# Two 8x8 triangular inverses at once, and the block below them by two products, in place of one 16-step substitution

## The chip, the cores and the metric

The kernel runs on one core of one Trainium2 chip. The time is device time in microseconds (us) from one launch, and the median of the runs is compared. Below, TensorE is PE, VectorE is DVE, ScalarE is ACT, GpSimd is POOL and SyncE, which issues most DMAs, is SP.

## The reference, cut to what matters

A two-layer decoder trunk on 256 tokens of width 1024. The first layer is a gated DeltaNet mixer with 8 heads of 128, the second an attention layer; each ends in a layer norm. The change lies in the first layer, where a unit lower-triangular system is solved for each head:

```python
lower = jnp.where(strict, jnp.einsum('nbhid,nbhjd->nbhij', k_beta, k) * decay, 0.0)
a_mat = jnp.eye(C) + lower
w = lax.linalg.triangular_solve(a_mat, k_beta * jnp.exp(gc)[..., None], left_side=True, lower=True, unit_diagonal=True)
u = lax.linalg.triangular_solve(a_mat, v * beta[..., None], left_side=True, lower=True, unit_diagonal=True)
```

The reference works in chunks of 64 tokens. The kernel works in two tiles of 128 tokens, which gives the same function, and so inverts a unit lower-triangular 128x128 matrix for each of 8 heads and 2 tiles, 16 in all.

## The kernel before, in words

**Work and stages.** The projections are the bulk of it. Weights arrive by DMA in units of 128x1024 (`raw`); ACT rounds each to a high part (`hi`), DVE computes the rest (`lo = raw - hi`), and PE multiplies three times (high by high, high by low, low by high). In order of time PE runs the first gate projection, keys and queries (`ps_kq`), values (`ps_v`) and gates (`ps_z`), the out projection of the first layer (`ps_y`, on the two halves `o0` and `o1` of the heads), and then the second layer (`ps_bv`, `ps_bkq`, `ps_bz`, `ps_y`). The chains of small work (convolution taps on DVE named `cv`, Gram matrices `ps_g`, transposes of the values `ps_vt`, the inverse and the solve) are woven between those matmuls.

**The inverse.** The 16 matrices form two groups of 8 (`inverse(0)`: heads 0 to 3, `inverse(1)`: heads 4 to 7). The 16x16 diagonal blocks come first: 8 matrices x 8 blocks = 64 blocks, one on each of 64 partitions, read from a scratch in DRAM into `mb` (POOL issues that DMA, `inv<-md`). `t16` begins as the identity; a loop over 15 columns `j` does one multiply and one add for each, an outer product of column `j` of the block with row `j` of `t16`, added below row `j`. Group 0 does this on POOL, group 1 on DVE (`INVERSE = [('gpsimd', 'p'), ('vector', 'v')]`). `t16` and its transpose (a copy into `tr[:, 1]`) go to DRAM by one SP DMA (`td`), and come back by eight SP DMAs into a layout of 32x32 blocks (`TC`, part of the tile `TR`). PE then joins blocks of 16 to 32 (`ps_x`, `ps_y`, 32x32 matmuls), 32 to 64 (`ps_x5`, `ps_y5`) and 64 to 128 (`ps_x6`, `ps_y6`, 64x64 matmuls); the profile prints these names without their numbers. For group 0 the 32-row copies `TR<-TR` and `TR<-ps_y` between those steps run on DVE, in the same queue as the 15-column loop of group 1.

**The solve.** `solve(grp)` multiplies by the inverse: `ps_s1`, copied to `Z` by ACT, `ps_s2`, an add on DVE, `ps_s3`, again a copy to `Z`. `read_out` makes `ps_o`, four sums of squares on ACT (`jk`), a power on POOL (`rs`), a scaled product on DVE (`og`), a transpose on PE (`ps_og`), and the high and low parts `o` on ACT and DVE. The out projection reads `o0` for the first 48 matmuls of the stage and then `o1`.

**What sets the order.** Each engine runs its own list in order. A planner writes these lists while the program is built: `Clock` keeps a modelled time for each engine and tile, and `Pipeline` issues a step of a chain between two matmuls when the model says that its inputs are there. For an instruction of the inverse the table says, n being the elements of its largest operand in one partition:

```python
cost = 480 + 1.2 * n     # POOL, two-input, output in inv
cost = 68 + scalars + n * (... 1.042)   # DVE
```

So any change of instructions or of `n` in the inverse changes what the planner puts where afterwards, on every engine. A semaphore guards each dependence; where the model is wrong, the engine that stands at the step waits. Before the first `ps_x` the planner adds a margin of `LATE = 1500` ns. A weight unit's DMA is issued on SP right behind the `lo` that frees its buffer, in the order in which the planner wrote them.

Of the kernel before, what the change touches and what calls it, by code (L numbers as in the profile page):

```python
# [20 lines left out]
ALU = mybir.AluOpType  # L21
# [205 lines left out]
class Pipeline:  # L227
# [12 lines left out]
    def at(self, e):  # L240
        return self.clock.t.get(self.ENGINES[e], START)
# [66 lines left out]
def body(ctx, tc, x, xt, cst_in, w0, wp, a_ln_g, a_ln_b, b_ln_g, b_ln_b, out):  # L308
# [360 lines left out]
    def gs_head(h):  # L669
# [41 lines left out]
        if n_md[h // 4] == 4:  # L711
            pipe.add(inverse(h // 4), R_INV)
# [8 lines left out]
    def inverse(grp):  # L721
        inv = act.tile([64, 4, 16, 16], F32, tag="ag" if grp == 0 else "ab", name=f"inv{grp}")
        mb, tr, prod = inv[:, 0], inv[:, 1:3], inv[:, 3]
# [9 lines left out]
        t16 = tr[:, 0]  # L733
# [4 lines left out]
                                        ap=[[16 * (P + 1), 64]] + list(blk.ap)))  # L738
        eng, e = INVERSE[grp]
        eng = getattr(nc, eng)  # L740
        yield e, [inv]
        for j in range(15):

            m, r = 15 - j, j + 1
            eng.tensor_mul(prod[:, 0:m, 0:r], mb[:, j, r:16].unsqueeze(2).to_broadcast([64, m, r]),
                           t16[:, j, 0:r].unsqueeze(1).to_broadcast([64, m, r]))
            eng.tensor_add(t16[:, r:16, 0:r], t16[:, r:16, 0:r], prod[:, 0:m, 0:r])
            if j in (4, 9):
                yield e, [t16]
        eng.tensor_copy(tr[:, 1], t16.rearrange("p a b -> p b a"))  # L750
        yield "t", [inv]
        nc.sync.dma_start(td[grp].rearrange("w q b r c -> (q b) w (r c)"),
# [507 lines left out]
```

## Time and profile before

| | |
|---|---|
| median of 3 runs | 301.84 us (301.78 to 303.9) |
| the profiled execution's own time | 302.44 us |
| its span, first to last instruction | 300.5 us |
| PE busy | 289.7 us (96%) |
| DVE busy | 210.2 us (70%) |
| ACT busy | 161.6 us (54%) |
| POOL busy | 51.2 us (17%) |
| granted TensorE clock, mean | 0.993 |

The span leaves 1.94 us of the execution's own time outside it, before the first and after the last instruction. "Busy" is the union of an engine's instructions; idle time of an engine counts only where another waits for it.

### The profile page before, as it was taken

The numbers are of one execution on the slowest core, as the hardware profiler recorded it, in microseconds if no ns is written. First come the engines' busy times: TensorE is split into PE (matmuls) and PEld (weight loads), VectorE is DVE, ScalarE is ACT, GpSimd is POOL, SyncE is SP. The second block draws the span as 40 slices with busy tenths as digits, with TensorE's granted clock in tenths as the row PEclk, the third lists the DMA queues.
The fourth block names the chain that finished last, engine by engine and source line by source line (L and its number), as shares of the span: only waits on it lengthen the run. The fifth ranks groups of instructions, "written<-read, shape, count | busy, mean of one in ns | idle before, by whom it ended". The sixth has DMA issues, their size and how long they took to land.

```text
span 300.5 us, 6569 instructions
## 1 busy us (share of the span) xinstructions
PE 289.7 (96%) x2598; PEld 266.7 (89%) x2598; DVE 210.2 (70%) x477; ACT 161.6 (54%) x329; POOL 51.2 (17%) x92
## 2 busy tenths in 40 slices
PE   8998999999999999999989999999999999999990
PEld 7898989989999989996878888899999999998890
DVE  0699479999999587687449893865655565763545
ACT  2588986635866552865352525775655558561000
POOL 8002310265884300110020010000000000000101
PEclk9999999999999999999999999999999999999997
DMA  6986505659576711336629055895444447400012
GB/s 224 377 278 223 177 17 176 214 165 316 189 258 182 235 61 29 93 127 209 201 108 328 2 179 172 256 313 199 143 129 153 144 143 273 142 0 2 0 70 71
DMA packets 19934, 49.43 MB, mean 164 GB/s; under 512 B 6304, under 2 KB 7968, under 8 KB 19904
## 3 DMA queue, kind: packets, MB, share of 16 engines
q1 hardware_dynamic: 18592, 46.73, 47.3%
q0 software_dynamic: 448, 1.18, 1.4%
q10 hardware_dynamic: 864, 1.11, 1.1%
q8 instruction: 20, 0.33, 0.5%
q14 instruction: 10, 0.08, 0.1%
HBM read 46.65 MB, written 2.36 MB: 163 GB/s over the span
## 4 chain that ended last, share of the span: by engine, by line
PE 77%; ACT 7%; DMA 5%; issue 5%; DVE 4%; ACTq 0%; POOL 0%; POOLq 0%; DVEq 0%; SPq 0%
PE ps_bkq L220 15%; PE ps_y L220 11%; PE ps_kq L220 9%; PE ps_v L220 8%; PE ps_bv L220 7%; PE ps_bz L220 7%; PE ps_z L220 5%; PE ps_g L220 4%; DMA raw<-in_wp_dram 4%; ACT ME L220 3%; DMA zraw<-in_w_dram 2%; PE ps_o L220 2%; PE ps_ot L220 2%; PE ps_sc L220 2%; PE ps_s L220 1%
## 5 line engine op out<-in xcount | busy, mean ns | idle before, releaser
L220 DVE TENSOR_TENSOR lo<-raw,hi 128x1024 fp32r<-128x1024 f32 (+1 forms) x79 | 94.6, 1207 | 10.1 <-ACT hi L220 9.9
L220 ACT CAST hi<-raw 128x1024 fp32r<-128x1024 f32 (+1 forms) x79 | 80.3, 1037 | 12.6 <-DMA raw<-in_wp_dram 6.5
L220 PE MATMUL ps_y<-hi,o 128*128 128x512 f32 (+1 forms) x144 | 43.5, 374 | 0.8 <-ACT o L220 0.7
L220 PE MATMUL ps_bkq<-x1h,hi 128*128 128x256 f32 x128 | 38.0, 297 | 0.0
L220 PE MATMUL ps_kq<-xh,hi 128*128 128x256 f32 x128 | 36.6, 286 | 0.0
L220 PE MATMUL ps_kq<-xh,lo 128*128 128x256 f32 x128 | 35.7, 279 | 0.0
L220 PE MATMUL ps_kq<-xl,hi 128*128 128x256 f32 x128 | 35.6, 278 | 0.0
L220 PE MATMUL ps_bkq<-x1l,hi 128*128 128x256 f32 x128 | 35.6, 278 | 0.0
L220 PE MATMUL ps_bkq<-x1h,lo 128*128 128x256 f32 x128 | 35.5, 278 | 0.0
L220 PEld LDWEIGHTS ps_y<-hi,o 128*128 128x128 f32 x144 | 25.9, 188 | 5.9 <-ACT o L220 1.2
L220 POOL TENSOR_TENSOR mv<-mv,nhalf 128x1 f32<-128x1 f32 x4 | 3.8, 951 | 135.0 <-DVE mv L220 135.0
L220 PE MATMUL ps_y<-lo,o 128*128 128x512 f32 (+1 forms) x72 | 26.3, 366 | 0.0
L220 DVE SCALAR_TENSOR_TENSOR cv<-ps_kq,cst_sb,cv 128x255 f32<-128x255 f32 (+2 forms) x48 | 21.5, 470 | 4.8 <-ACT cv L220 4.6
L220 PEld LDWEIGHTS ps_bkq<-x1h,hi 128*128 128x128 f32 x128 | 24.1, 189 | 0.2
L220 PEld LDWEIGHTS ps_bkq<-x1l,hi 128*128 128x128 f32 x128 | 24.1, 188 | 0.2
L220 PEld LDWEIGHTS ps_kq<-xh,hi 128*128 128x128 f32 x128 | 24.3, 190 | 0.0
L220 PEld LDWEIGHTS ps_kq<-xh,lo 128*128 128x128 f32 x128 | 24.0, 188 | 0.1
L220 PEld LDWEIGHTS ps_kq<-xl,hi 128*128 128x128 f32 x128 | 24.1, 188 | 0.0
L220 PEld LDWEIGHTS ps_bkq<-x1h,lo 128*128 128x128 f32 x128 | 24.1, 188 | 0.0
L220 PE MATMUL ps_v<-xh,hi 128*128 128x256 f32 x64 | 18.7, 292 | 0.0
L220 PE MATMUL ps_bz<-x1h,hi 128*128 128x256 f32 x64 | 18.0, 282 | 0.0
L220 PE MATMUL ps_v<-xl,hi 128*128 128x256 f32 x64 | 17.9, 280 | 0.0
(177 smaller groups left out, 676.6 us busy)
## 6 DMA issues: line engine op xcount, KB each, us to landing
raw<-in_wp_dram SPq DMA_DIRECT2D x77, 512.0 KB, 4.2
md<-ME POOLq DMA_DIRECT2D x8, 128.0 KB, 2.6
late<-in_x_dram SPq DMA_DIRECT2D x1, 1024.0 KB, 4.9
zraw<-in_w_dram ACTq DMA_DIRECT2D x4, 136.0 KB, 4.3
zraw<-in_w_dram ACTq DMA_DIRECT2D x2, 272.0 KB, 4.8
x_sb<-in_xt_dram SPq DMA_DIRECT2D x4, 128.0 KB, 4.1
x_sb<-in_xt_dram SPq DMA_DIRECT2D x2, 256.0 KB, 5.0
raw<-in_wp_dram SPq DMA_DIRECT2D x2, 256.0 KB, 4.1
```

Of the source, the lines that this page charges most:

```text
L220: r = f(*args, **kw)
```

## The change: 8-blocks side by side, then the block below

Each 16x16 block is split into its two 8x8 diagonal blocks and the 8x8 block below. The substitution now runs over 7 columns, and each multiply and add works on both 8-blocks at once (a stride of 136 elements, 8 rows and 8 columns on). The lower left block of the inverse is then the product of the lower inverse, the block of the matrix, and the upper inverse: two 8x8 products inside each partition. Each is one multiply of 8x8x8 = 512 elements into `p8`, and a sum over the last 8: on DVE (group 1) one `tensor_reduce`, on POOL (group 0) three adds of 256, 128 and 64 elements. The temporary begins at `tr[:, 1]` and reaches into the plane behind it, which alone was the temporary (`prod`) before. Behind the block nothing is changed in the code.

```diff
-        for j in range(15):
-            m, r = 15 - j, j + 1
-            eng.tensor_mul(prod[:, 0:m, 0:r], mb[:, j, r:16].unsqueeze(2).to_broadcast([64, m, r]),
-                           t16[:, j, 0:r].unsqueeze(1).to_broadcast([64, m, r]))
-            eng.tensor_add(t16[:, r:16, 0:r], t16[:, r:16, 0:r], prod[:, 0:m, 0:r])
-            if j in (4, 9):
+        def at(t, row, col, *dims):
+            return bass.AP(tensor=t.tensor, offset=t.offset + 16 * row + col, ap=[t.ap[0]] + [list(d) for d in dims])
+        wide = tr[:, 1]
+        for j in range(7):
+            m, r = 7 - j, j + 1
+            pv = at(wide, 0, 0, (m * r, 2), (r, m), (1, r))
+            tv = at(t16, r, 0, (136, 2), (16, m), (1, r))
+            eng.tensor_mul(pv, at(mb, j, r, (136, 2), (1, m), (0, r)), at(t16, j, 0, (136, 2), (0, m), (1, r)))
+            eng.tensor_add(tv, tv, pv)
+            if j == 3:
                 yield e, [t16]
+        p8 = at(wide, 0, 0, (64, 8), (8, 8), (1, 8))
+        for out, left, right in ((at(mb, 8, 0, (16, 8), (1, 8)), at(mb, 0, 8, (1, 8), (0, 8), (16, 8)),
+                                  at(t16, 0, 0, (0, 8), (1, 8), (16, 8))),
+                                 (at(t16, 8, 0, (16, 8), (1, 8)), at(t16, 8, 8, (16, 8), (0, 8), (1, 8)),
+                                  at(mb, 8, 0, (0, 8), (1, 8), (16, 8)))):
+            eng.tensor_mul(p8, left, right)
+            yield e, [inv]
+            if e == "v":
+                eng.tensor_reduce(out, p8, axis=mybir.AxisListType.X, op=ALU.add)
+            else:
+                for w in (4, 2, 1):
+                    d = at(wide, 0, 0, (64, 8), (8, 8), (1, w)) if w > 1 else out
+                    x0, x1 = (at(wide, 0, k, (64, 8), (8, 8), (1, w)) for k in (0, w))
+                    if w == 1:
+                        x0, x1 = (at(wide, 0, k, (64, 8), (8, 8)) for k in (0, 1))
+                    eng.tensor_add(d, x0, x1)
+            yield e, [inv]
```

On POOL, the loop of group 0. Its end before, from the second of the two `md` DMAs that POOL issues inside the loop:

```order
L220 DMA md<-ME 128x2x128
L220 TENSOR_TENSOR inv_843<-inv_843 64x5x11 x2
L220 TENSOR_TENSOR inv_843<-inv_843 64x4x12 x2
L220 TENSOR_TENSOR inv_843<-inv_843 64x3x13 x2
L220 TENSOR_TENSOR inv_843<-inv_843 64x2x14 x2
L220 TENSOR_TENSOR inv_843<-inv_843 64x15 x2
L220 COPY inv_843<-inv_843 64x256
```

and now, from the last column to the end of the first product:

```order
L220 TENSOR_TENSOR inv_843<-inv_843 64x14
L220 TENSOR_TENSOR inv_843<-inv_843 64x2x7
L220 TENSOR_TENSOR inv_843<-inv_843 64x512
L220 DMA md<-ME 128x2x128
L220 TENSOR_TENSOR inv_843<-inv_843 64x64x4
L220 TENSOR_TENSOR inv_843<-inv_843 64x64x2
L220 TENSOR_TENSOR inv_843<-inv_843 64x8x8
```

The multiply of 512 and the three adds come once more behind this, and then the same copy. There are 22 two-input instructions where there were 30, and two `md` DMAs stand inside them before and now.

On DVE, where the loop of group 1 (`inv`) and the copies of group 0's inverse (`TR_845`) share the queue. Before:

```order
L220 TENSOR_TENSOR lo_1489<-raw_1244,hi_1488 128x1024
L220 TENSOR_TENSOR inv_1359<-inv_1359 64x15 x2
L220 TENSOR_TENSOR inv_1359<-inv_1359 64x14x2 x2
L220 TENSOR_TENSOR inv_1359<-inv_1359 64x13x3 x2
L220 TENSOR_TENSOR inv_1359<-inv_1359 64x12x4 x2
L220 TENSOR_TENSOR inv_1359<-inv_1359 64x11x5 x2
L220 COPY TR_845<-TR_845 32x8x32 x6
L220 COPY TR_845<-ps_y_1636 32x8x32 x2
L220 TENSOR_TENSOR inv_1359<-inv_1359 64x10x6 x2
```

and now, from the eighth instruction of the loop:

```order
L220 TENSOR_TENSOR inv_1354<-inv_1354 64x2x4x4
L220 TENSOR_TENSOR lo_1482<-raw_1231,hi_1481 128x1024
L220 COPY TR_845<-TR_845 32x8x32 x6
L220 TENSOR_TENSOR inv_1354<-inv_1354 64x30
L220 TENSOR_TENSOR inv_1354<-inv_1354 64x2x3x5
L220 TENSOR_TENSOR inv_1354<-inv_1354 64x24
L220 TENSOR_TENSOR inv_1354<-inv_1354 64x2x2x6
L220 TENSOR_TENSOR inv_1354<-inv_1354 64x14
L220 TENSOR_TENSOR inv_1354<-inv_1354 64x2x7
L220 TENSOR_TENSOR inv_1354<-inv_1354 64x512
L220 COPY TR_845<-ps_y_1633 32x8x32 x2
L220 TENSOR_REDUCE inv_1354<-inv_1354 64x8x8
```

A `lo` has gone behind the first eight instructions of the loop, and between the two kinds of copies of group 0 there are now seven instructions of the loop, where there was none. After the end of the loop three `cv` taps stand between its last four instructions.

On PE, where the out projection passes from the first half of the heads to the second (the tile numbers tell `o0` from `o1`). Before:

```order
L220 MATMUL ps_o_2261<-Z_2207,ME_162 128x128 x8
L220 MATMUL ps_og_2275<-ident_121,og_2270 128x128 x4
L220 MATMUL ps_y_2235<-hi35_1627,o0_1772 128x512
L220 MATMUL ps_y_2235<-lo35_1628,o0_1772 128x512
L220 MATMUL ps_y_2235<-hi35_1627,o0_1772 128x512
L220 MATMUL ps_y_2066<-hi36_1706,o1_2208 128x512
```

and now:

```order
L220 MATMUL ps_s3_2225<-W_175,TR1_1356 128x128 x4
L220 MATMUL ps_y_2203<-hi35_1617,o0_1752 128x512
L220 MATMUL ps_y_2203<-lo35_1618,o0_1752 128x512
L220 MATMUL ps_y_2203<-hi35_1617,o0_1752 128x512
L220 MATMUL ps_o_2250<-Z_2196,ME_162 128x128 x8
L220 MATMUL ps_og_2271<-ident_121,og_2266 128x128 x4
L220 MATMUL ps_y_2056<-hi36_1683,o1_2197 128x512
```

The last three matmuls on `o0` have moved ahead of `ps_o`, and `ps_og` is followed at once by a matmul on `o1`. Between group 1's `ps_s1` and the first matmul on `o1` there are 12 matmuls on `o0` now, and were 18 before: six more stand ahead of `ps_s1`.

The other moves, as counts. PE has the same matmuls as before and in the same order up to the values' projection and from the attention layer's first projection on. Group 0's first `ps_x` has six projection matmuls fewer ahead of it, its `ps_x6` twelve more. The transpose `ps_vt` that stood right ahead of group 1's `ps_x6` now stands 39 projection matmuls ahead of it. On SP one more `raw` load stands between `td` and the eight loads of `TC`, for each group. On DVE and ACT one weight unit is split earlier, so that one more `lo` stands in the stretch of POOL's loop.

## Rows read from the trace of the kernel before

**Rows 1.** The page's part 1: engine, busy us, share of the span, instructions.

```profile
PE 289.7 (96%) x2598; PEld 266.7 (89%) x2598; DVE 210.2 (70%) x477; ACT 161.6 (54%) x329; POOL 51.2 (17%) x92
```

**Rows 2.** Stretches: us; busy PE, PEld, DVE, ACT, POOL; granted clock, DMA share, GB/s.

```profile
70.00:89.40 19.40, 19.40 (x156) 18.33 (x156) 18.32 (x38) 13.20 (x22) 17.10 (x34) 1.00 0.74 250
...
120.00:160.00 40.00, 38.59 (x519) 33.13 (x518) 26.09 (x52) 22.86 (x66) 4.05 (x4) 1.00 0.49 162
```

**Rows 3.** Timeline of POOL, its loop: start, us, instructions [idle before <-releaser].

```profile
70.08 5.78 POOL L220 TENSOR_TENSOR inv<-inv 64x15 f32<-64x15 f32 x10 [4.62 <-DMA inv<-md]
75.80 0.75 POOL L220 DMA_DIRECT2D md<-ME  x1
...
88.69 0.61 POOL L220 COPY inv<-inv 64x256 f32<-64x256 f32 x1
```

**Rows 4.** POOL's loop by shapes, 70 to 90 us: busy us, mean ns.

```profile
L220 POOL TENSOR_TENSOR inv<-inv 64x28 f32<-64x28 f32 x4 | 0.9, 235 | 0.3
...
L220 POOL TENSOR_TENSOR inv<-inv 64x64 f32<-64x64 f32 x2 | 0.6, 299 | 0.2
```

**Rows 5.** All of `inv`'s instructions: ns min/median/max, first and last start.

```profile
L220 POOL TENSOR_TENSOR inv<-inv x30: 212/293/1248, 70.1 to 88.4; 64x15 f32<-64x15 f32 x4, 64x28 f32<-64x28 f32 x4, 64x39 f32<-64x39 f32 x4, 64x48 f32<-64x48 f32 x4
L220 DVE TENSOR_TENSOR inv<-inv x30: 167/201/219, 104.3 to 113.9; 64x15 f32<-64x15 f32 x4, 64x28 f32<-64x28 f32 x4, 64x39 f32<-64x39 f32 x4, 64x48 f32<-64x48 f32 x4
```

**Rows 6.** Two-input instructions of DVE by shapes, whole span: busy us, mean ns.

```profile
L220 DVE TENSOR_TENSOR lo<-raw,hi 128x1024 fp32r<-128x1024 f32 x77 | 93.3, 1220 | 9.9 <-ACT hi L220 9.7
...
L220 DVE TENSOR_TENSOR W<-ps_s,W 128x512 f32<-128x512 f32 x2 | 1.4, 692 | 3.6 <-PE ps_s L220 3.6
```

**Rows 7.** DVE in 104 to 115.5 us by shapes: busy us, mean ns.

```profile
L220 DVE TENSOR_TENSOR inv<-inv 64x28 f32<-64x28 f32 x4 | 0.7, 180 | 0.1
```

**Rows 8.** Timeline of SP's queue: group 0's inverse out to DRAM and back.

```profile
89.33 0.69 SPq L220 DMA_DIRECT2D td<-inv  x1
91.73 0.35 SPq L220 DMA_DIRECT2D raw<-in_wp_dram  x1
92.85 4.01 SPq L220 DMA_DIRECT2D TR<-td  x8
```

**Rows 9.** DMAs into `TR`: us from issue to landing, min/median/max.

```profile
DMA to landing us min/median/max: 2.0/2.1/2.8
```

**Rows 10.** Timeline of PE: group 0's first joining step, and its third.

```profile
100.80 0.75 PE L220 MATMUL ps_x<-TR,ME 32*32 32x32 f32 x64
...
109.90 1.14 PE L220 MATMUL ps_x<-TR,ME 64*64 64x64 f32 x16
```

**Rows 11.** Timeline of DVE: loop of group 1 and copies of group 0.

```profile
104.32 2.24 DVE L220 TENSOR_TENSOR inv<-inv 64x15 f32<-64x15 f32 x10 [0.59 <-DMA inv<-md]
106.48 1.61 DVE L220 COPY TR<-TR 32x256 f32<-32x256 f32 x6
108.44 0.87 DVE L220 COPY TR<-ps_y 32x256 f32<-32x256 f32 x2 [0.35 <-PE ps_y L220]
```

**Rows 12.** Timeline of PE: group 1's solve, and the passage to `o1`.

```profile
139.76 0.44 PE L220 MATMUL ps_vt<-ident,cv 128*128 128x128 f32 x2 [0.38 <-ACT cv L220]
...
145.36 1.05 PE L220 MATMUL ps_s<-W,TR 128*128 128x128 f32 x8
...
152.40 1.95 PE L220 MATMUL ps_o<-Z,ME 128*128 128x128 f32 x16
...
156.22 0.50 PE L220 MATMUL ps_y<-hi,o 128*128 128x512 f32 x1 [0.74 <-ACT o L220]
...
157.00 0.73 PE L220 MATMUL ps_y<-hi,o 128*128 128x512 f32 x2
```

**Rows 13.** Timeline of ACT: the copy of group 1's second `Z`.

```profile
151.21 0.59 ACT L220 COPY Z<-ps_s 128x512 f32<-128x512 f32 x1 [0.39 <-PE ps_s L220]
```

**Rows 14.** The chain of waits, in order of time: runs of projection matmuls.

```profile
159.33 8.24 PE ps_y L220 x36
...
255.74 15.66 PE ps_bz L220 x138
```

## The prediction

> **What bounds the kernel now.** I read the busy times first. PE is busy 289.7 of 300.5 us, DVE 210.2 and POOL 51.2 [rows 1]. A shorter chain on DVE or POOL is therefore worth only what PE waits for it. The stretches come next: PE is busy all 19.40 us in which POOL runs its loop, and 38.59 of 40.00 us from 120 to 160, where group 1 is inverted and solved [rows 2]. So the 16x16 loops delay nothing by themselves, and at most 1.41 us of PE idle time stands where a better order could remove it. Last I read the timelines at the points where PE meets the inverse, to see how long its input had been there. For group 0, `td` is issued at 89.33, the eight loads of `TC` from 92.85 to 96.86 [rows 8], each landing 2.1 us after its issue [rows 9], so by 98.96 at the latest; PE takes the first `ps_x` at 100.80 [rows 10]. That is 1.8 us of room. Group 1's solve is the tight place: PE waits 0.38 us for a `ps_vt` at 139.76, and 0.74 us for `o` at 156.22 [rows 12].
>
> **The change, part by part.**
>
> *POOL, group 0.* Before, 30 two-input instructions and two `md` DMAs take from 70.08 to the copy at 88.69, 18.6 us [rows 3]. Unhindered instructions lie between 0.212 us (the shortest) [rows 5] and 0.299 us (64 elements) [rows 4], about 0.265; with gaps of 0.08 (0.3 us for four) [rows 4] and 0.75 for each DMA [rows 3] that makes 30 x 0.345 + 1.5 = 11.9 us. The other 6.7 us are long cases, up to 1.248 us [rows 5], which is the length of a `lo` on DVE, 1.220 [rows 6]: I read them as POOL held back until a `lo` ends, some seven times 1 us. Now 14 instructions have 14 to 32 elements, 0.225 each, 3.15 us. For the long ones no row exists. The line through 0.235 at 28 and 0.299 at 64 elements [rows 4] rises by 1.78 ns for each element and gives 1.10 us at 512, 0.64 at 256, 0.41 at 128 and 0.30 at 64: 2.45 us for a product, 4.9 for both. As bounds I take 0.61 us (the copy of 256 elements) [rows 3] and twice the line. With 22 gaps (1.8) and the two DMAs (1.5) the chain is 11.3 us unhindered, only 0.6 less than before: the work saved in the loop comes back in the sums. The seven holds stay, and one more `lo` stands in the stretch, so the end lies between 0.6 us earlier and 0.4 later. I take it as unchanged. The planner, whose table gives 480 + 1.2n, takes 2.7 us off, and so it puts `ps_x` six projection matmuls earlier: 6 x 0.1135 (15.66 us for 138 of them [rows 14]) = 0.7, to 100.1. Room shrinks from 1.8 to 1.1 us. On SP one more `raw` load now stands ahead of the `TC` loads; its `lo` is the one whose load was issued at 91.73 before [rows 8], ahead of 92.85, so it costs nothing. Sum: 0.
>
> *DVE, group 1.* Ten instructions took 2.24 us [rows 11], 0.22 to 0.24 each with their gap (median 0.201 [rows 5]), 6.9 us for 30. Now 14 small ones at 0.18 [rows 7] and 0.03 of gap are 2.9 us, and four of 512 elements at 0.692 [rows 6] and gap 2.9: 5.8 us, 1.1 less. A `tensor_reduce` has no row; it is bounded by 0.219 (64 elements) [rows 5] and 1.220 (1024) [rows 6], and I take the two-input value of 512, nearest in size. PE does not wait for this chain: DVE is free 1.08 of 19.40 us [rows 2] in the busiest stretch and more later.
>
> *Group 0's copies behind that loop.* They run on DVE in the queue between loop pieces. The loop cannot begin before its data land, near 104.3 [rows 11]. Then: eight instructions 1.7, the `lo` that moved behind them 1.1, the six copies 1.6 [rows 11], six instructions 1.3, the multiply of 512 0.7, and the first of the copies out of `ps_y`, 0.42 (half of 0.87 [rows 11]): 111.1 us. Before it was 108.9. PE's `ps_x6` stands twelve matmuls later now, 109.90 [rows 10] + 1.4 = 111.3. It just fits: 0 us, and 0.5 lost if the multiply costs 1.220.
>
> *Group 1's solve.* PE's work up to the first matmul on `o1` is the same, in another order. The `ps_vt` wait goes with the earlier place of `ps_vt` (about 0.5 us from the end of the matmul before it to its start). But six matmuls on `o0` stand ahead of `ps_s1` now instead of behind it: 6 x 0.229 (8.24 for 36 [rows 14]) = 1.4. So `ps_s1` comes at 145.36 [rows 12] + 1.4 - 0.5 = 146.2. The second `Z` was ready at 151.80 [rows 13], 6.4 us behind it, and is now at 152.65. Before, `ps_o` stood at 152.40 [rows 12], 0.6 behind `Z`, 7.04 us and fifteen matmuls on `o0` after `ps_s1`; with twelve between them PE arrives 7.04 - 3 x 0.229 = 6.35 us after `ps_s1`, at 152.55, and goes on at 152.7. From `ps_o` the chain through ACT (squares, `o`) and DVE takes as long as before, 156.22 - 152.40 = 3.8 us to the first and 4.6 to the third matmul on `o1` [rows 12]; the third comes at 157.3 instead of 157.00. The three matmuls that filled this wait stand ahead of it. So the gain at `ps_vt` turns into a longer wait at `o1`, and 0.35 us more are lost. From there the order is the same and PE is the bound.
>
> Sum: 0 + 0 + 0 + 0.35. The profiled execution took 302.44 us (300.5 of span and 1.94 around it), so 302.8 for it; that execution lies 0.6 above the median of the runs shown, 301.84, from which I predict **302.2 us**. A change under 1%, 3.0 us, can't be told from none here.
>
> **The rivals.**
>
> *Nothing but a better order (0.10).* The loops are shorter in instructions, the planner's picture of DVE comes closer to the chip, and the idle time of 1.41 us [rows 2] goes: 301.84 - 1.4 = 300.4. For it: 1.1 us less on DVE. Against it: the passage to `o1` has lost its filling matmuls. The Trainium skill, "VectorE: DVE Perf Modes", section "Rules for kernel authors", advises fewer instructions, which would favour this case; it has no bearing on an engine that nobody waits for.
>
> *POOL's chain comes late (0.11), the slower side.* If the long instructions cost up to twice the line, from an extrapolation over eight times the size or because each meets a `lo`, the chain is 4.9 us longer. From 1.1 us on PE waits at the first `ps_x`, with all later matmuls behind it in its list: 4.9 - 1.1 = 3.8, so up to 301.84 + 0.35 + 3.8 = 306.0, middle 304.1. For it: all earlier holds were a whole `lo` long. Against it: the number of `lo`s, not of POOL instructions, sets the number of holds.
>
> *DVE is held back by POOL (0.10).* The trace shows POOL waiting for a `lo`, 1.248 against 0.299 us [rows 4, 5]. Should it go the other way too, the two products' 4.9 us stand in DVE's way, where POOL's instructions were short before. Half of it met by a `lo` is 2.45; less DVE's 1.08 us to spare [rows 2] leaves 1.4 late, for which PE waits at the Gram matmuls: 301.84 + 0.35 + 1.4 = 303.6. No row shows such a hold. The Trainium skill, "SBUF — State Buffer", section "SBUF: two separate sides", has VectorE and GpSimd share a port pair that the first to start holds for its whole instruction while the other is blocked. By that rule this case is what must come; the trace bears out one direction of it.
>
> **How the numbers follow.** The forecast gets 0.69, with 301.2 to 302.9 as its own range (0.6 us either way for POOL's end and the 0.5 of the multiply, and the spread of the runs). The 8-in-10 range takes the gain almost to its end and the two slow cases past their middles: **300.6 to 304.5**. Faster by over 1% (below 298.8) lies beyond all of PE's idle time here: 0.03. Slower by over 1% (above 304.9) is the upper half of the POOL case and a little of the others: 0.08. Within 1%: 0.89.
>
> **What would show it.** POOL: 14 instructions near 0.23 us, products near 1.1, and the copy at 88 to 89.3. PE: `ps_x` near 100.1 with no wait on a DMA; no wait at `ps_x6` near 111.3; no wait at a `ps_vt` near 139; a wait of 1.2 to 2 us in all ahead of and among the first matmuls on `o1`, the third of them near 157.3. `lo` stays at 1.22 us with no idle time ahead of it where a product runs. A DMA wait at `ps_x`, or `lo`s that begin late beside POOL's products, would make the prediction wrong, and so would a `tensor_reduce` far above 0.7 us.

## The result, and the profile after

The changed kernel takes 306.28 us (median of four runs, 304.91 to 307.04) against 302.05 for the kernel before: 1.0145 times as long, 95% interval 1.012 to 1.0169. It is slower by 4.2 us, where 302.2 was forecast and 304.5 was the upper end of the range. Here and below a ratio leaves out runs that lie over 1.5% above the fastest of their kernel; medians and ranges keep them. The profiled execution is the fastest of the four: 304.91 us, 303.2 of span. First its busy times, as in [rows 1].

```profile
PE 289.5 (95%) x2598; PEld 266.3 (88%) x2598; DVE 212.9 (70%) x465; ACT 161.8 (53%) x329; POOL 53.3 (18%) x84
```

PE has the same work; the 2.7 us of span are PE's idle time. The view of stretches says where (columns as in [rows 2]):

```profile
10.00:60.00 50.00, 49.58 (x382) 46.02 (x381) 42.61 (x117) 39.91 (x89) 10.02 (x13) 1.00 0.60 203
...
70.00:89.40 19.40, 17.24 (x135) 15.97 (x135) 19.26 (x35) 10.42 (x18) 16.60 (x25) 1.00 0.71 229
89.40:101.00 11.60, 11.60 (x102) 11.29 (x103) 9.89 (x24) 7.80 (x19) 5.56 (x6) 1.00 0.82 214
101.00:120.00 19.00, 18.54 (x409) 17.42 (x409) 14.87 (x41) 10.24 (x20) 0.57 (x1) 1.00 0.25 70
120.00:160.00 40.00, 37.63 (x518) 32.75 (x518) 22.74 (x45) 21.04 (x63) 4.52 (x4) 1.00 0.46 140
```

Length minus PE's busy time is what PE stands idle. The last column is a second profiled execution of the same change (after_again, 305.99 us), which the first experiment gave:

| stretch, us | before | after | after_again |
|---|---|---|---|
| 10 to 60 | 1.02 | 0.42 | 0.58 |
| 70 to 89.4 | 0 | 2.16 | 1.82 |
| 101 to 120 | 0.03 | 0.46 | 1.54 |
| 120 to 160 | 1.41 | 2.37 | 2.30 |
| sum | 2.46 | 5.41 | 6.24 |

PE's waits in the changed kernel by what ended them (us in total, times, longest):

```profile
PE ps_g L220 <- ACT kq L220: 2.2, 1, 2.2
PE ps_y L220 <- ACT o L220: 1.4, 1, 1.4
...
PE ps_y L220 <- issue: 0.7, 1, 0.7
...
PE ps_y L220 <- ACT X L220: 0.4, 1, 0.4
PE ps_vt L220 <- ACT cv L220: 0.2, 1, 0.2
```

The largest, at the Gram matmuls `ps_g`, is followed back through ACT to DVE. This is POOL by shapes while it runs its loop, 68 to 87.5 us (busy us, mean ns), which answers to [rows 4]:

```profile
L220 POOL TENSOR_TENSOR inv<-inv 64x512 f32<-64x512 f32 x2 | 4.7, 2354 | 0.2
...
L220 POOL TENSOR_TENSOR inv<-inv 64x256 f32<-64x256 f32 x2 | 1.7, 835 | 0.1
L220 POOL TENSOR_TENSOR inv<-inv 64x128 f32<-64x128 f32 x2 | 1.7, 828 | 0.2
...
L220 POOL TENSOR_TENSOR inv<-inv 64x64 f32<-64x64 f32 x2 | 0.6, 298 | 0.2
```

And this is DVE's timeline beside the two products, which ran from 76.9 to 79.1 and from 82.5 to 85.1 us:

```profile
77.53 2.63 DVE L220 TENSOR_TENSOR lo<-raw,hi 128x1024 fp32r<-128x1024 f32 x1
...
83.62 1.51 DVE L220 SCALAR_TENSOR_TENSOR cneg<-cneg,beta 128x2 f32<-128x2 f32 x1
...
86.50 0.47 DVE L220 SCALAR_TENSOR_TENSOR cv<-ps_kq,cst_sb,cv 128x253 f32<-128x253 f32 x1
```

A `lo` takes 2.63 us instead of 1.220 [rows 6]. `cneg<-cneg,beta`, two elements a partition, takes 1.51 us; in the trace of before it took 0.17 (all of its instructions in 70 to 89 us: ns min/median/max, first and last start):

```profile
L220 DVE SCALAR_TENSOR_TENSOR cneg<-cneg,beta x2: 167/168/169, 70.8 to 83.2; 128x2 f32<-128x2 f32 x2
```

`cneg` ends 0.02 us behind the product beside it, and the `lo` 1.1 us behind, which is about its own length. Together DVE is held 2.75 us; it had 1.08 us to spare in this stretch [rows 2] and now has 0.14. The key's last convolution tap comes at 86.50, ACT's `kq` ends at 87.48, and PE goes on at 87.53 after 2.16 us. So POOL and DVE hold each other: [rows 5] showed POOL waiting for a `lo`, this is the other direction.

On DVE itself the loop of group 1 by shapes (104 to 117 us) is:

```profile
L220 DVE TENSOR_TENSOR inv<-inv 64x512 f32<-64x512 f32 x2 | 2.1, 1054 | 0.1
L220 DVE TENSOR_REDUCE inv<-inv 64x64 f32<-64x512 f32 x2 | 1.3, 672 | 0.0
L220 DVE TENSOR_TENSOR inv<-inv 64x30 f32<-64x30 f32 x4 | 0.7, 182 | 0.1
```

The sum over 512 elements costs about what was priced (0.67 against 0.692). The product of 512 with strided and broadcast operands costs 1.054, half as much again as the plain one of [rows 6].

### The profile page after: what moved, and what is told of

It is laid out like the page before. It is cut to its first block, busy times and chain, and to the rows that moved or that the text cites. A ratio compares the mean times of both kernels' runs of the same rounds, so it can differ in the third digit from the quotient of the medians.

```text
span 303.2 us, 6549 instructions
## 1 busy us (share of the span) xinstructions
PE 289.5 (95%) x2598; PEld 266.3 (88%) x2598; DVE 212.9 (70%) x465; ACT 161.8 (53%) x329; POOL 53.3 (18%) x84
## 4 chain that ended last, share of the span: by engine, by line
PE 69%; DVE 12%; issue 7%; DMA 5%; ACT 3%; POOL 2%; ACTq 0%; POOLq 0%; DVEq 0%; SPq 0%
PE ps_bkq L220 15%; PE ps_y L220 13%; PE ps_kq L220 8%; PE ps_bv L220 7%; PE ps_bz L220 7%; DVE lo L220 4%; PE ps_z L220 4%; PE ps_g L220 3%; DVE cv L220 2%; PE ps_sc L220 2%; PE ps_o L220 2%; PE ps_ot L220 2%; DMA zraw<-in_w_dram 2%; DMA raw<-in_wp_dram 2%; PE ps_s L220 1%
## 5 line engine op out<-in xcount | busy, mean ns | idle before, releaser
L220 DVE TENSOR_TENSOR lo<-raw,hi 128x1024 fp32r<-128x1024 f32 (+1 forms) x79 | 96.5, 1228 | 13.9 <-ACT hi L220 13.7
```

The lines of the kernel that those rows point to most:

```text
L220: r = f(*args, **kw)
```

## The experiments

Fifteen kernels. Each is timed against the kernel before on the same chip; ratios have their 95% interval.

### New arithmetic or new order

The planner orders the work by modelled costs, so the change does two things: other instructions in the loop, and another order of everything around it. To separate them the planner is told the cost of the other loop. A list of forced costs makes a piece of the loop last in the model as long as the piece it stands for (the first instruction gets the sum, the rest take back what the model adds for a dependence):

```diff
+            if self.force:
+                cost = self.force.pop(0)
             end = start + cost
...
+        def as_if(sizes, k):
+            one = (lambda n: 480 + 1.2 * n) if e == "p" else (lambda n: 68 + 1.042 * n)
+            total = sum(one(n) for n in sizes) + 130 * (len(sizes) - 1)
+            nc.force[:] = [total] + [-130] * (k - 1)
# frozen, first piece of the new loop:
+        as_if([(15 - j) * (j + 1) for j in range(0, 5) for _ in range(2)], 8)
# order, first piece of the old loop:
+        as_if([2 * (7 - j) * (j + 1) for j in range(0, 4) for _ in range(2)], 10)
```

`frozen` is the new arithmetic, yielding where the old loop did, with the old loop's costs; PE, ACT and SP keep the order of before row for row. `order` is the old loop with the new loop's costs and yields, so PE, ACT and SP have the order of the change. `dve_only` has the new arithmetic for group 1 (`if grp == 1:`), the old loop for group 0 and the planner's own, third, order. `after_again` is the change once more.

> The changed kernel once more, since its four runs lay at 304.9 to 307.0 and the profile shows the lowest of them. Both theories: 304.9 to 307.0 us. If the port theory (POOL's 512-element products hold up DVE's two-input and small instructions, and PE then waits for a convolved key) is right, the spread comes from where a product meets a lo, and a slower execution shows longer holds or a longer wait of PE ahead of ps_g or after the first ps_x than the 2.2 us of the profile at hand.

> The new arithmetic on both engines in the old order: the planner is given the old loop's modelled cost, so that PE, ACT and SP have the list of the kernel before, row for row, and DVE and POOL differ in the loop's instructions alone. Port theory: a lo beside each product takes about 2.5 us instead of 1.22, the key's last tap comes 1 to 2.5 us later, and PE waits for it at ps_g: 303 to 305 us. Order theory (the planner's new order is what costs): 301.8 to 302.6 us, and no wait at ps_g.

> The old arithmetic in the new order: the planner is given the new loop's modelled cost, so that PE, ACT and SP have the changed kernel's list, row for row, and DVE and POOL differ in the loop's instructions alone. Port theory: no lo over 1.3 us, no wait of 2 us at ps_g; what stays is the longer wait at the passage to o1, 0.4 to 1 us: 302.4 to 303.2 us. Order theory: 304.5 us or more.

> The new arithmetic for group 1 (DVE) alone, the old loop for group 0 (POOL); the planner is free. Port theory: POOL has no long instruction, so no lo over 1.3 us and no wait at ps_g: 301.6 to 302.8 us, with the multiplies of 512 still at 1.05 us. Order theory: the time follows the order that the planner finds, which is neither of the two, so it may lie anywhere from 302 to 306.

| | median us (range, runs) | ratio |
|---|---|---|
| after_again | 305.99 (305.37 to 306.12, 4) | 1.0132 [1.0102, 1.0162] |
| frozen | 303.36 (302.2 to 304.35, 10) | 1.0051 [1.0031, 1.007] |
| order | 305.17 (304.36 to 307.54, 4) | 1.0119 [1.0057, 1.0182] |
| dve_only | 303.09 (301.09 to 306.37, 10) | 1.0034 [0.9999, 1.0069] |

Before stood at 301.70. The order alone costs 3.5 us (by its interval 1.7 to 5.5), the arithmetic alone 1.7, both together 4.3. That this is less than the sum is within the noise of `order`. `after_again` came out in its range, but the profile is not as expected: the wait at `ps_g` is shorter than in the first (1.82 us), and 1.54 us by "issue" at 105.30 are new. In `dve_only`, with a spread of 5 us, the profiled execution has two waits of PE by "issue" (1.9 us together) and none at `ps_g`. Both parts had to be followed.

### The hold between POOL and DVE

`frozen_pool` and `frozen_dve` are `frozen` with the new arithmetic for one group alone (`if grp == 0:` and `if grp == 1:` around it, the old loop under `else:`), both in the order of before.

> The order of before, its loop on POOL for group 0, and the new arithmetic on DVE for group 1 alone. Theory A, the 1.5 us of frozen are the hold between the long products on POOL and DVE: none of it is left here, no wait at ps_g over 0.3 us, and 301.9 us (301.3 to 302.5). Theory B, they are DVE's two strided products of 1.05 us and what they push back: 303.2 us (302.6 to 303.9) with a longer wait at o or at ps_vt.

> The order of before, the new arithmetic on POOL for group 0 alone, and the loop of before on DVE for group 1. Theory A, the hold: an instruction of DVE of 1.4 us or more beside a 64x512 product where the same form takes 0.2 or 1.2, a wait of 0.5 to 2 us at ps_g, and 303.2 us (302.5 to 304). Theory B, the strided products on DVE make the 1.5 us of frozen: 301.9 us (301.3 to 302.5).

Measured: `frozen_dve` 302.59 us, 0.9995 [0.9972, 1.0018]; `frozen_pool` 304.55 us, 1.0058 [1.004, 1.0076]. Before stood at 302.90 there, 1.2 higher than beside `frozen`, so the ratios are to be read and not the times: theory A, on both sides. DVE's dearer products cost nothing; POOL's long ones make the whole of `frozen`'s price. The holds in `frozen_pool`, DVE's timeline:

```profile
77.20 2.30 DVE L223 TENSOR_TENSOR lo<-raw,hi 128x1024 fp32r<-128x1024 f32 x1
...
82.96 1.43 DVE L223 SCALAR_TENSOR_TENSOR cneg<-cneg,beta 128x2 f32<-128x2 f32 x1
```

The second product runs beside `cneg` from 82.82 to 84.37 us (POOL by shapes, 82 to 84.3 us):

```profile
L223 POOL TENSOR_TENSOR inv<-inv 64x512 f32<-64x512 f32 x1 | 1.5, 1549 | 0.1
```

This is near its own length. The first product takes 2.11 to 2.15 us in all six profiles that have it. The second takes 1.54 in `frozen` and 1.55 here, and 2.46 to 2.56 in the four profiles in the order of the change, where a `lo` was already running when it began: there POOL waits first, and DVE behind it.

What PE waits for, first in `frozen_pool` and then in `frozen_dve`:

```profile
PE ps_g L223 <- ACT kq L223: 1.8, 1, 1.8
...
PE ps_y L223 <- ACT o L223: 0.7, 1, 0.7
```

```profile
PE ps_y L223 <- ACT o L223: 0.7, 1, 0.7
...
PE ps_g L223 <- ACT kq L223: 0.2, 1, 0.2
```

Then the cure that this suggests: on POOL, products and additions cut so that no instruction has more than 64 elements, in the order of before (`frozen_cut`) and in that of the change (`after_cut`).

```diff
-            eng.tensor_mul(p8, left, right)
+            pieces(eng.tensor_mul, 8, p8, left, right)     # on POOL: 8 of 64 elements
...
-                    eng.tensor_add(d, x0, x1)
+                    pieces(eng.tensor_add, w, d, x0, x1)
```

> The new arithmetic in the order of before (as in frozen, 303.4 us), with every product and addition of over 64 elements on POOL cut into pieces of 64: 28 more instructions on POOL, nothing moved on PE, ACT, DVE and SP. Theory A, a long instruction on POOL holds VectorE's instruction beside it and so the key's chain: no lo beside POOL over 1.5 us, the wait at ps_g (0.7 us) under 0.4, PE idle 0 to 0.3 us in 70 to 89.4, and 302.2 us (301.5 to 302.8). Theory B, the 1.5 us of frozen come from something else (the strided instructions on DVE, the scatter of fetches): 303.4 us (302.9 to 304).

> The changed kernel in its own order, with every product and addition of over 64 elements on POOL cut into pieces of 64. Theory A, the hold of long POOL instructions makes the wait of 1.8 to 2.2 us at ps_g: that wait is 0 to 0.4, and what is left is the price of the order (order: 305.2 us): 304.9 us (304.0 to 305.7). If the stall at ps_g gave the later steps time, the waits behind 100 us grow by as much and it is 305.5 to 306. Theory B, the wait at ps_g is the order's, not the hold's: it stays at 1.8 to 2.2 and the time at 306.0 us (305.4 to 306.6).

Measured: `frozen_cut` 307.79 us, 1.0177 [1.0119, 1.0235]; `after_cut` 309.95, 1.0248 [1.0207, 1.0288]. The mechanism came as theory A had it: in 70 to 89.4 us PE stands 0.02 and 0.08 us, no longer 0.66 (in `frozen`, whose profile is the fastest of its ten runs) to 2.16. The time was a plain miss in both, since POOL's own chain was left out. There are 22 more instructions on POOL, not the 28 of the expectation. POOL by shapes in `frozen_cut`:

```profile
L223 POOL TENSOR_TENSOR inv<-inv 64x64 f32<-64x64 f32 x30 | 14.8, 526 | 0.3
...
L223 POOL COPY inv<-inv 64x256 f32<-64x256 f32 x1 | 0.6, 632 | 0.1
```

Most pieces of 64 elements take 0.28 to 0.44 us, five take 1.3 to 1.5 and one 0.61; in the mean 0.526. Eight pieces in the place of one product are thus 2.2 to 3.5 us even where nothing holds them, instead of 1.54 to 2.15. Holds are the smaller part of what this adds in `frozen_cut`: seven of the chain's two-input instructions take over 0.9 us there, and six did in `frozen` beside the two products (nine in `after_cut`, against five in the change). The chain up to its copy grows from 18.1 to 22.4 us (24.9 in `after_cut`), the inverse reaches DRAM late, and PE waits where the rival on POOL's chain had put it:

```profile
PE ps_x L223 <- DMA TR<-td: 3.0, 3, 2.2
```

In `after_cut` it is 4.0 us. Behind these waits the clock falls, which makes a further part of the time (the stretch of `frozen_cut`, granted clock third from the end; in `after_cut` it is 0.82 too, in `frozen` 1.00):

```profile
101.00:120.00 19.00, 16.47 (x363) 15.14 (x364) 10.03 (x29) 6.84 (x11) 0.00 (x0) 0.82 0.39 120
```

Long instructions on POOL hold DVE; short ones no longer hold it (no `lo` beside them takes over 1.42 us in `frozen_cut`), but they take POOL longer.

### The fetch of PE's own instructions

What the new order costs was still dark: in `order` no other engine is late enough for 3.5 us; the wait at `o` is 1.44 us, 0.7 more than before. Its trace has a wait in the middle of group 0's 32x32 matmuls that no semaphore ended ("issue"):

```profile
103.36 0.19 PE L223 MATMUL ps_y<-XI,TR 32*32 32x32 f32 x1
105.41 0.22 PE L223 MATMUL ps_y<-XI,TR 32*32 32x32 f32 x3 [1.86 <-issue]
```

The DMA part of the page lists a queue that the kernel does not issue to (in before: packets, MB, share of 16 engines):

```profile
q8 instruction: 20, 0.33, 0.5%
```

These are 20 packets of 16 KB, one for every 260 of PE's weight loads and matmuls. I read them as PE's program, fetched while it runs. By the packets' own records the sixth comes at 98.5 us in before, and at 103.3 in `order` and 103.0 in `after_again`, behind the packets of two weight loads. Counted in PE's instructions it is the same: in 14 of the 17 profiles the sixth packet starts when PE has begun 1,427 to 1,467 weight loads and matmuls, whatever the kernel, and only in `order`, `after_again` and `before_m24` (below) later, at 1,608 to 1,689. In before PE meets some 480 of them in the 5 us from the first `ps_x` on (`ps_x` and `ps_y` of group 0, a matmul about every 8 ns). In `order` and `after_again` it runs out there, and goes on 2.15 and 2.3 us after the start of that packet. The order of the change has the first `ps_x` six matmuls earlier: 1,463 weight loads and matmuls start ahead of it in the profile instead of 1,475, so the burst lies 12 instructions nearer to the place at which the packet is asked for.

The test moves the edges alone, that is the places in the program at which one block of 16 KB ends and the next begins, by PE's warm-up, for whose result nothing waits. The planner does not see the added instructions, and the time of those taken away is put back in its model. `_p40` and `_p16` put 40 or 16 instructions more there, `before_p216` 216, `before_m24` 24 fewer; every later block then begins that much earlier or later in the program, and no other instruction moves against another. The edits, shortened:

```diff
         for _ in range(n):
             nc.tensor.matmul(ps_warm[:, 0:P], ones, ones, start=True, stop=True)
# p40: one of these calls fewer, and 11 of 32x32 (p16: one fewer and 5; p216: four fewer and 58)
+        for _ in range(11):
+            tc.nc.tensor.matmul(ps_warm[0:32, 0:32], ones[0:32, 0:32], ones[0:32, 0:32], start=True, stop=True)
# m24: one of these calls in place of nine, and
+        for _ in range(2):
+            tc.nc.tensor.matmul(ps_warm, ones, ones[:, 0:1].to_broadcast([P, 512]), start=True, stop=True)
```

> The loop of before in the order of the changed program (as in order, 305.2 us), and 40 more instructions on PE ahead of everything: ten more matmul calls of 32x32 in the warm-up (11 added, one of 128x128 taken away), so that every later 256-instruction block of PE's program begins 40 instructions earlier; no instruction after the warm-up moves against another. Theory A, the fetch of PE's own instructions: in the trace of order a 16 KB instruction packet came at 103.3 us instead of 98.5 as in before, behind two weight loads, and PE stood 1.9 us in the middle of group 0's 32x32 matmuls. Its block is now due some 2 us earlier, ahead of those loads: the packet at 95 to 98 us, no wait of over 0.5 us at ps_y by issue near 105, and 303.3 us (302.8 to 304.0). Theory B, the data of the joining come late in the new order: nothing changes, 305.2 us (304.4 to 306.0), and the 1.9 us stand where they stood.

> The kernel before, with nothing changed but PE's warm-up: 58 calls of 32x32 added and four of 128x128 taken away, 216 instructions more, so that every later block of 256 begins 216 instructions earlier in the program, or 40 later. Theory A: the block that was due at 98.3 us and fetched at 98.5 is due at about 100.7, when two weight loads (packets until 103.5 in the trace of before) stand ahead of it: the packet at about 104, PE idle 1 to 3 us among group 0's 32x32 matmuls by issue, and 303.5 us (302.7 to 304.7). Theory B: where a block of instructions begins does not matter, 301.7 us (301.2 to 302.3).

> The changed kernel with 40 more instructions in PE's warm-up (11 calls of 32x32 added, one of 128x128 taken away), nothing else moved: its blocks of 256 instructions begin 40 earlier, as in order_p40. Theory A, the changed kernel loses time to the fetch of PE's instructions in some executions (a wait of 1.5 us by issue at ps_y near 105 us in the trace of after_again, none there in the first trace): the packet comes at 95 to 98 us, that wait is gone, and 304.9 us (304.2 to 305.6). Theory B, the waits at ps_g and at o make all of it: 306.0 us (305.4 to 306.8).

> The kernel before with the same 40 instructions in PE's warm-up: the control of order_p40 and after_p40. If the added calls only fill the wait for the first weights: 302.0 us (301.4 to 302.6), and no wait of over 0.5 us by issue. If the place of the blocks costs or gives something by itself in this kernel too, it is over 1 us away from 302.0, and the packet that was at 98.5 us stands at about 96.4.

> The kernel before with a warm-up of PE of three calls (one of 128x128 and two of 128x512 columns) in place of nine of 128x128: as long, but 24 instructions fewer, so that each later block of 256 begins 24 instructions later in the program. Theory A, the fetch: the block that was requested about 98.3 us is requested at about 99.8, when the packets of two weight loads are under way (98.5 to 103.5 us in the trace of before); its packet comes at 103 to 104 us, PE has run its instructions out at about 103.1 and waits 1.5 to 3.5 us by issue among group 0's 32x32 matmuls until 2.2 to 2.9 us behind the packet's start; 304.8 us (303.5 to 306). Theory B: no wait there, 302.3 us (301.7 to 302.9).

> The old loop in the new order, with 16 more instructions in PE's warm-up (five calls of 32x32 added, one of 128x128 taken away): the block is requested about 0.9 us earlier than in order. Theory A: its packet at 97 to 99.5 us, ahead of the weight loads that SP issues at 98.9 us, no wait of over 0.7 us by issue at ps_y near 105, and 303.8 us (303.0 to 304.8), 1 to 2 less than order. Theory B: 305.2 us (304.4 to 306.2), the wait where it was.

> The changed kernel with the same 16 instructions. Theory A: the packet at 97 to 99.5 us, no wait of over 0.7 us by issue at ps_y near 105, the waits at ps_g (1.8 to 2.4) and at o (1.4) as they were, and 305.2 us (304.4 to 306.0). Theory B, the fetch has no part in the changed kernel's time: 306.2 us (305.5 to 307).

| | median us (range, runs) | ratio | packet | waits by issue, us |
|---|---|---|---|---|
| before_m24 | 306.30 (306.13 to 307.38, 4) | 1.0155 [1.012, 1.0191] | 102.4 | 2.15 at `ps_y` |
| before_p40 | 305.69 (302.42 to 307.91, 10) | 1.007 [1.0039, 1.0101] | 95.6 | 0.88 and 0.96 at `ps_x` |
| before_p216 | 310.91 (310.26 to 314.21, 4) | 1.0314 [1.0252, 1.0376] | 107.9 (the seventh) | 2.58 at `ps_y` |
| order_p40 | 304.41 (304.1 to 306.26, 6) | 1.0085 [1.0052, 1.0118] | 96.4 | 0.46 and 0.28 at `ps_x` |
| order_p16 | 305.38 (302.31 to 307.3, 10) | 1.01 [1.006, 1.0139] | 97.6 | none |
| after_p40 | 307.37 (306.37 to 308.34, 4) | 1.0153 [1.0117, 1.0188] | 98.7 | 0.27 and 0.74 at `ps_x` |
| after_p16 | 306.67 (306.16 to 308.2, 4) | 1.0169 [1.0128, 1.0209] | 101.5 | 0.6 at `ps_y` |

The packet is the sixth, at its start in us, where nothing else is said. `before_m24` is the cleanest: the kernel before, with nothing changed but the warm-up and so the edges, loses 4.7 us. PE's timeline at the wait:

```profile
104.89 0.23 PE L220 MATMUL ps_y<-TR,XI 32*32 32x32 f32 x4 [2.15 <-issue]
```

Its DMA queues from 102 to 103.5 us (packets, MB, share), the first stretch after 98 in which the instruction queue appears:

```profile
q1 hardware_dynamic: 16, 0.04, 9.4%
q8 instruction: 1, 0.02, 5.2%
```

The wait is where theory A put it, 2.5 us behind the packet's start, and in the predicted size. The time came out 1.5 above the expectation, and the stretches of its PE say why (granted clock third from the end):

```profile
101.00:104.00 3.00, 1.74 (x66) 1.50 (x66) 1.61 (x2) 1.75 (x2) 0.00 (x0) 1.00 0.42 139
104.00:107.00 3.00, 2.11 (x80) 1.92 (x80) 1.92 (x11) 0.59 (x1) 0.00 (x0) 0.93 0.52 180
107.00:110.00 3.00, 3.00 (x42) 2.86 (x42) 1.46 (x7) 1.61 (x4) 0.00 (x0) 0.50 0.02 5
```

Behind the wait the clock stands at 0.50, the 1.2 GHz level, for three microseconds (1.00 there in before); PE is busy 291.4 us in all instead of 289.7. `before_p216` shows the same wait (2.58 us) but carries some 5 us more from the start, where its 58 calls took 6.4 us in place of about 2: that part was not foreseen and is not evidence. In `order_p40` and `order_p16` the packet came when it was expected and the wait near 105 us is gone. Their medians are 304.41 and 305.38 where 303.3 and 303.8 were expected, so by time alone the cure is not shown: the freed execution of `order_p16` meets `ps_x6` 0.94 us ahead of the copies of `TR` on DVE instead. `before_p40`, the control, loses time to these edges too (1.007): its two waits of 0.9 us stand at 105.59 and 135.71, 2.7 and 2.9 us behind their packets, the seventh and a later one.

`after_p40` and `after_p16` were misses. Their first `ps_x` comes 3.2 us later than in `order_p40` and `order_p16` (2.4 and 1.9 us of it are the wait at `ps_g`), so the packet is late too (98.7 and 101.5); neither waits at `ps_y` near 105 us, yet neither is faster. What costs them more is behind the wait at `ps_g`. PE's stretch from 88 to 92 us in `after_p16`, and then in the first profile of the change:

```profile
88.00:92.00 4.00, 4.00 (x15) 3.23 (x16) 3.96 (x12) 1.99 (x4) 0.47 (x1) 0.59 0.58 195
```

```profile
88.00:92.00 4.00, 4.00 (x31) 3.65 (x30) 3.96 (x12) 2.24 (x5) 0.12 (x1) 1.00 0.71 199
```

15 matmuls instead of 31 in four microseconds: after the same wait the clock fell in one execution and not in the other. From the matmul that ends the wait to the first `ps_x` the same work takes 14.9 us in `after_p16` and 14.8 in `after_p40`, and 13.4 in both profiles of the change: 1.4 us more.

## Why the prediction was wrong

The steps that failed are the hold (put at nothing) and the price of the new order (put at 0.35 us, with nothing for the fetch of PE's instructions); the clock, and a late group of copies, add to them.

- **"The seven holds stay ... I take it as unchanged."** POOL's loop as a whole did come out unchanged, 18.3 us from 68.48 to the copy at 86.81 against 18.6. That was partly luck. The product was priced at 1.10 us by a line through short instructions and took 2.15 and 2.56. By `frozen_pool` 1.5 us of this are its own cost, not a hold (2.11 and 1.55 there against twice 1.10), so the holds on POOL must have been that much shorter than the seven that were added. And the step looked only at POOL's end: the same overlap held DVE by 1.4 and 1.3 us. The rival "DVE is held back by POOL" is the right mechanism at the right place, 2.16 us for PE at the Gram matmuls where 1.4 was priced. The hold itself was sized about right, 2.45 us (half of the products' 4.9) against 2.75; what was too much is the 1.08 us of spare time on DVE that were taken off, of which only 0.6 counted. In `frozen_pool` it is the same: 2.34 held, 1.76 waited. It got 0.10 because no row showed that direction. The Trainium skill, "SBUF — State Buffer", section "SBUF: two separate sides", states it: the one that starts first keeps the shared port pair for the whole instruction. By that rule the hold was certain, and `frozen_pool` agrees (1.43 us for `cneg`, 2.30 for a `lo`).
- **"On SP one more `raw` load now stands ahead of the `TC` loads ... it costs nothing."** The eighth `TC` load left SP at 97.80 instead of 96.42, and the landings took 3.2 to 4.9 us from their issue instead of 2.0 to 2.8 [rows 9]. The room of 1.1 us at `ps_x` was used up, at a cost of 0.2 us to the weight load there. Whether the later place of these loads also brings the weight loads behind them and the packet together was not tested apart.
- **The new order's price was put at 0.35 us in all; `order` measured 3.5.** The passage to `o1` was right: no wait at a `ps_vt` near 139, and 1.43 us where 1.2 to 2 were expected [rows 12]; with what `ps_vt` gives back it costs 0.3 us more than before, and 0.35 was forecast. The first of group 0's copies out of `ps_y` ended near 112.0 instead of 111.1: 0.57 us because the loop began at 104.87 and not at 104.3, 0.3 from the product of 1.05. PE's `ps_x6` did not wait for it, as forecast, but came at 112.11; PE waits 0.37 us one step on, for `X`, which ACT copies late because its own copy `TR<-ps_y` waits until 112.52 for DVE's copies and a `cv` and a `hi` stand between the two. That path was not looked at. Missing altogether was the fetch of PE's instructions, 1.86 us in `order`, 1.54 and 0.64 in `after_again` and 0.66 at 134.65 in the first profile. The Trainium skill, "Runtime: NRT & Kernel Launch", section "Instruction fetch mechanics", has the instruction memory refilled in blocks of 16 KB and the cost of crossing one mostly hidden. The packets here agree in size; in the bursts of 32x32 matmuls the cost is not hidden.
- **The clock was not in the sum.** In the first profile of the change it did not fall; in `after_p16` and `after_p40` a wait of 1.9 to 2.4 us was followed by 1.4 us more for the same work (4 us at a granted 0.59 are 1.6 lost). Why it falls in some executions and not in others stays open.

For the changed kernel this makes, from the four profiles of it and its shifted twins: 1.8 to 2.4 us at `ps_g`, in two of the four 1.4 more of clock behind it; 0.7 more at `o`; 0.6 to 2.2 of fetch and copies among the joining's matmuls. What stays open is how these are spread over the executions, and how much of the new order's 3.5 us is the fetch: the packet's place cures the wait in the traces, but no time on record shows the gain. Each build has one profile, and the runs of `order_p16` alone lie between 302.3 and 307.3 us. Nor was it tried to put the weight loads behind the instruction packet, since SP's order is the planner's. No version beat the kernel before; the nearest, `frozen_dve`, equals it.

## What to carry to other kernels

Before one long GpSimd instruction replaces many short ones, look at what VectorE does beside it: the hold goes both ways, and cutting the long one into pieces freed VectorE here but made GpSimd's own chain 4 to 7 us longer. A planner's cost table is part of the change: measure the old arithmetic in the new order and the new arithmetic in the old order before explaining anything. In a kernel with bursts of hundreds of tiny matmuls, differences of 1% can come from where the instruction blocks begin, so a control that moves only those belongs to such a comparison.

## What the runs showed of the hardware

- A 128x2 instruction of VectorE beside a 64x512 product on GpSimd: 1.51 and 1.43 us instead of 0.17; a `lo` 2.63 and 2.30 instead of 1.22.
- A 64x512 product on GpSimd with strided and broadcast operands: 2.11 to 2.15 us (the first) and 1.54 (the second, in `frozen` and `frozen_pool`); eight pieces of it 0.28 to 0.44 us each where nothing holds them.
- A 64x512 product on VectorE with strided and broadcast operands: 1.05 us; the plain 128x512 one 0.692; the sum of 512 down to 64 elements 0.67.
- Fifteen waits of TensorE by "issue" (0.4 to 2.6 us, in twelve of the 17 profiles) ended 2.15 to 2.9 us after a 16 KB instruction packet started, each in or behind a burst of matmuls about 8 ns apart.
- The sixth of these packets starts after 1,427 to 1,467 of TensorE's weight loads and matmuls in 14 of the 17 profiles, and after 1,608 to 1,689 in the three where it stood behind weight loads.
- 24 instructions fewer in the warm-up cost the kernel before 4.7 us (in its profile 2.15 of wait, and PE busy 1.7 longer, with the clock at 0.50 for three microseconds).
- Of four waits of 1.8 to 2.4 us at `ps_g` in the change and its shifted twins two were followed by a granted clock of 0.59 and 0.66 over four microseconds, two by 1.00.
